# Two tiles for the blocks of w_down, loaded a unit ahead, the sums of g in the gate's places, and the sums pinned in program order on VectorE

## The chip, the core and the metric

The kernel runs on one core of one Trainium2 chip. The metric is the device time of one execution, in microseconds (us); lower is better. The kernel before takes 1152.91 us (median of 3 runs, 1152.59 to 1155.61). The engines are called as in the profile: PE is TensorE, PEld its weight loads, DVE is VectorE, ACT is ScalarE, POOL is GpSimd, SP is SyncE, which here issues all the DMAs from one queue, in order.

## What is computed

The reference runs one encoder layer on two sequences of 512 tokens (plus 16 meta tokens): a convolution branch and an attention branch, a projection `w_out`, and a gated feed-forward network (FFN). The change lies in the FFN alone:

```python
hf = _rms(h, ffn_norm_g[i])
h = h + (jax.nn.silu(hf @ w_gate[i]) * (hf @ w_up[i])) @ w_down[i]
```

`hf` has 1024 rows (tokens) and 1024 columns, `w_gate` and `w_up` are 1024 x 2816, `w_down` is 2816 x 1024. Everything is float32; the kernel gets that accuracy out of three matmuls on a high and a low part of each operand (`mm3`, L151).

## The kernel before

**Stages.** Projections and the convolution, attention, `w_out`, and then the FFN, in two parts: the *units* (gate and up), and the *down* products.

**Seven products in place of eight.** Each pair of 128-wide blocks of FFN columns is a 2 x 2 block product, and the kernel computes such a product by a scheme of Strassen's kind with 7 block products. It needs sums of the blocks of both operands. For a pair `p` (there are 11) unit `2p` makes the gate part `silu(hf @ w_gate)` and unit `2p+1` the up part, which is multiplied by the gate part at once; so there are 22 units of 7 products, 12 matmuls of 512 columns each. Before each product the block of weights or its sum is split into a high part (ACT, L962) and a low part (POOL, L964), in tiles `wc`; the sums of weight blocks themselves are made on DVE (L946, tiles `tt`, four of them). Each product leaves PE in a PSUM bank (`pt`, four of them), is read from there by ACT (L975) or DVE (L979, L981, L983, L993, L997) and so frees its bank; L998 multiplies by the gate part. `raw`, `h_...64` and a part of `slots` are the places to which the weights of gate and up units are loaded, two units ahead (L938).

**Sums for the down products.** The down product is done in the same way, with operands `g` (the result of gate and up) and `w_down`. Their sums are made while the units run, and go to DRAM:

- `g_sums(p, j)` (from L1003) runs in the up unit of pair `p`, and makes the sums of the four blocks of g: three written to the tiles `hf0` and `hf1` (`hf2` in the code, free since the FFN's transposes), one in place. DMAs store them to `d_a11s1`, `d_a12a22`, `d_s3s2` and `d_s4`.
- `w_sums(p, r, j)` (from L1021) handles the blocks of `w_down` for pair `p`, one half of the columns at a time (`r` = 0 in the up unit, `r` = 1 in the next pair's gate unit). One round is: load four 128 x 256 blocks into the tile `wt` (two DMAs, L1031), make four sums in place on DVE (L1035, L1037, L1040, L1042), store two of the blocks to `d_t1t3` (L1038) and two to `d_t4t2` (L1043). There are 22 rounds, and there is one `wt`: it has the place of the tile for the norm's gain (`tag="gain", bufs=1`), so that a round's loads wait for the stores of the round before.

**What sets the order.** The program is written for the Tile framework. Its scheduler places every instruction on its engine's queue by a simulation of the time at which its inputs are there, by what is ready, with the order of the program as the tie-break. The queue itself then runs strictly in order, and so does SP's queue of DMAs. The sums of `w_down` depend on nothing but their own loads, so that the scheduler may put them far ahead of the place in which the program has them. A place to which something is loaded or written is only waited for by semaphores; nothing else limits how far ahead it may be.

**Down products.** After the units, 77 steps of 12 matmuls read the stored sums back (L1117, L1118), split them (ACT L1129, DVE L1130) and multiply. They are split four steps ahead of their use and loaded eight steps ahead of that; the last units already prepare the first ones.

## Time and profile before

| | |
|---|---|
| Median of 3 runs | 1152.91 us (1152.59 to 1155.61) |
| Profiled execution: its own time | 1156.38 us |
| Profiled execution: span, first to last instruction | 1154.6 us |
| Granted TensorE clock, mean | 0.984 |
| PE busy, whole span | 1089.3 us (94%) |
| DVE busy, whole span | 837.4 us (73%) |
| DMA, mean | 127 GB/s |
| First load of `wt` and last one issued | 480.18 us, 726.02 us |
| Units: first product read from PSUM, last unit's first one | 468.22 us, 921.83 us |

How to read it: a line of the group view has the line of the kernel, the engine, the operation, what it writes and reads, the shape, the count, and then the busy time, the mean duration of one in ns, and the idle time just before with what ended it. A line of the timeline has the start, the duration, and in brackets the idle time of the engine before it. A row of the view by windows has, for each engine, its busy time in that stretch with the number of instructions, then the granted clock of PE (1.00 is full), the share of the DMA engines and the bytes moved. `xN` is always a count.

### The profile page before, as it was taken

How to read it: one execution, taken by the hardware profiler on the slowest of the kernel's cores; microseconds unless marked ns; L12 is line 12 of the kernel's file. 1: busy time of each engine (PE TensorE's matmuls, PEld its weight loads, DVE VectorE, ACT ScalarE, POOL GpSimd, SP SyncE). 2: the span in 40 equal slices, each digit the busy share in tenths (PEclk: the TensorE clock that was granted, in tenths of full speed). 3: DMA queues.
4: the chain of work that ended last, by engine and by line, in shares of the span. 5: the costliest groups of instructions: out<-in, count | busy, mean ns of one | idle time of the engine just before them, and what ended most of it. 6: DMA issues, size and time to landing. Idle time of an engine off the chain costs nothing.

```text
span 1154.6 us, 15888 instructions
## 1 busy us (share of the span) xinstructions
PE 1089.3 (94%) x5874; PEld 935.1 (81%) x5874; DVE 837.4 (73%) x1197; ACT 499.0 (43%) x832; POOL 471.5 (41%) x409
## 2 busy tenths in 40 slices
PE   5999998999999999789798998999999999999997
PEld 4999887888878999777576776888888888888886
DVE  5599997888887548997658678867675584756643
ACT  6455525786874525632221221333223344533431
POOL 6389736563652313583443434554554400000002
PEclk9999999999989999899998999999999999999999
DMA  8211111010111312445465465443314389765513
GB/s 277 76 38 41 42 52 55 25 56 1 38 37 64 120 37 92 139 143 183 140 216 193 144 209 170 150 137 117 120 39 135 126 308 369 250 224 183 183 37 127
DMA packets 71421, 147.06 MB, mean 127 GB/s; under 512 B 6944, under 2 KB 29728, under 8 KB 71344
## 3 DMA queue, kind: packets, MB, share of 16 engines
q1 hardware_dynamic: 71344, 146.06, 37.7%
q8 instruction: 46, 0.75, 0.3%
q14 instruction: 31, 0.25, 0.1%
HBM read 105.92 MB, written 40.11 MB: 126 GB/s over the span
## 4 chain that ended last, share of the span: by engine, by line
PE 59%; DVE 21%; DMA 12%; issue 3%; ACT 2%; POOL 1%; SPq 1%; DVEq 0%; POOLq 0%; ACTq 0%
PE pt L151 41%; PE ps L151 12%; DMA wt<-in_w_down_dram 5%; DMA d_t4t<-wt 5%; DVE ps L329 3%; DVE ps L337 3%; PE pt L645 2%; PE pt L615 2%; DVE pacc L339 1%; DVE wt L1037 1%; DVE wt L1035 1%; DVE tt L946 1%; DVE wt L1042 1%; DVE hf L879 1%; DMA raw<-in_w_in_dram 1%
## 5 line engine op out<-in xcount | busy, mean ns | idle before, releaser
L151 PE MATMUL pt<-act_h,wc 128*128 128x512 f32 (+1 forms) x552 | 178.2, 385 | 7.6 <-DVE slots L997 5.9
L964 POOL TENSOR_TENSOR wc<-tt,wc 128x512 fp32r<-128x512 f32 x84 | 114.9, 1386 | 99.2 <-ACT wc L962 78.0
L151 PE MATMUL pt<-hn_h,wp 128*128 128x256 f32 (+2 forms) x576 | 132.8, 324 | 1.1 <-ACT hn_h L141 1.1
L151 PEld LDWEIGHTS pt<-act_h,wc 128*128 128x128 f32 x552 | 104.2, 191 | 29.9 <-DVE slots L997 5.5
L176 POOL TENSOR_SCALAR ms<-ms 128x1 f32<-128x1 f32 (+1 forms) x24 | 12.8, 534 | 250.5 <-ACT re L175 213.8
L151 PE MATMUL pt<-act_l,wc 128*128 128x512 f32 (+1 forms) x276 | 106.3, 385 | 3.4 <-DVE act_l L898 3.4
L151 PEld LDWEIGHTS pt<-hn_h,wp 128*128 128x128 f32 x576 | 97.3, 192 | 10.1 <-ACT hn_h L141 1.5
L1130 DVE TENSOR_TENSOR re<-re,re 128x1024 fp32r<-128x1024 f32 x53 | 64.2, 1223 | 47.2 <-ACT re L1129 46.8
L151 PE MATMUL pt<-hn_l,wp 128*128 128x256 f32 (+2 forms) x288 | 93.6, 326 | 0.0
L137 POOL TENSOR_TENSOR wp<-raw,wp 128x1024 fp32r<-128x1024 f32 x28 | 69.2, 2472 | 54.9 <-ACT wp L134 54.8
L962 ACT CAST wc<-tt 128x512 fp32r<-128x512 f32 x88 | 51.2, 616 | 78.6 <-PE pt L151 69.9
L1129 ACT CAST re<-re 128x1024 fp32r<-128x1024 f32 x53 | 55.2, 1054 | 68.0 <-PE ps L151 23.8
L151 PE MATMUL pt<-re 128*128 128x512 f32 x360 | 84.0, 389 | 0.0
L151 PEld LDWEIGHTS pt<-re 128*128 128x128 f32 x360 | 67.6, 188 | 14.0
L964 POOL TENSOR_TENSOR wc<-raw,wc 128x512 fp32r<-128x512 f32 x30 | 42.1, 1419 | 79.8 <-ACT wc L962 79.8
L151 PE MATMUL pt<-a12h,wc 128*128 128x512 f32 (+1 forms) x184 | 63.7, 411 | 10.7 <-DVE slots L997 10.6
L151 PE MATMUL pt<-wp,act_h 128*128 128x256 f32 x384 | 71.4, 285 | 1.6 <-DVE h L842 1.5
L590 POOL TENSOR_SCALAR p<-p,sst 128x512 f32<-128x512 f32 x64 | 44.1, 693 | 69.3 <-DVE sst L588 61.3
L151 PE MATMUL pt<-s4h,wc 128*128 128x512 f32 (+1 forms) x184 | 60.1, 390 | 6.7 <-DVE h L979 6.7
L151 PEld LDWEIGHTS pt<-act_l,wc 128*128 128x128 f32 x276 | 53.0, 192 | 13.5 <-DVE act_l L898 3.6
L151 PE MATMUL ps<-re 128*128 128x512 f32 x276 | 63.9, 389 | 0.0
L151 PEld LDWEIGHTS pt<-wp,act_h 128*128 128x128 f32 x384 | 60.1, 192 | 2.2 <-DVE h L842 1.7
(283 smaller groups left out, 2895.8 us busy)
## 6 DMA issues: line engine op xcount, KB each, us to landing
raw<-in_w_gate_dram SPq DMA_DIRECT2D x22, 512.0 KB, 4.2
wt<-in_w_down_dram SPq DMA_DIRECT2D x44, 256.0 KB, 3.3
re<-in_w_down_dram SPq DMA_DIRECT2D x31, 256.0 KB, 4.6
raw<-in_w_in_dram SPq DMA_DIRECT2D x12, 512.0 KB, 3.8
slots<-in_w_up_dram SPq DMA_DIRECT2D x11, 512.0 KB, 3.7
d_t1t<-wt SPq DMA_DIRECT2D x22, 256.0 KB, 2.5
h<-in_w_up_dram SPq DMA_DIRECT2D x11, 512.0 KB, 5.7
d_t4t<-wt SPq DMA_DIRECT2D x22, 256.0 KB, 2.8
```

The source lines that it names most:

```text
L137: nc.gpsimd.tensor_sub(lo[:, a], raw[:, a], hi[:, a].bitcast(F32))
L151: nc.tensor.matmul(out_ap, lhsT=w_, rhs=m_, start=first and i + j == 0, stop=last and i == n - 1 and j == 2)
L176: nc.gpsimd.tensor_scalar(ms[:rows], ms[:rows], EPS, 0.0, op0=ALU.add, op1=ALU.add)
L329: nc.vector.scalar_tensor_tensor(a_, half_win(c, 0, i, HS + 1), k, a_, ALU.mult, ALU.add)
L337: nc.vector.scalar_tensor_tensor(m_, both[:, :, i:i + HS], k, m_, ALU.mult, ALU.add)
L590: nc.gpsimd.tensor_scalar(pr[:, real], pr[:, real], st[:, 2, t:t + 1], 1.0, op0=ALU.mult, op1=ALU.mult)
L615: nc.tensor.transpose(pt[:, t * 128:(t + 1) * 128], self.ps[t][:, n0:n0 + w], ident)
L645: nc.tensor.matmul(self.po, lhsT=v, rhs=p_, start=self.done + j == 1, stop=self.done + j == 5)
L962: nc.scalar.copy(w[:, 0:512], src)
L964: lo_eng.tensor_sub(w[:, 512:1024], src, w[:, 0:512].bitcast(F32))
L1129: nc.scalar.copy(w[:, :, LO], blocks[n])
L1130: nc.vector.tensor_sub(w[:, :, HI], blocks[n], w[:, :, LO].bitcast(F32))
```

## The change

- The blocks of `w_down` are loaded to `hf0` (rounds with `r` = 0) and `hf1` (`r` = 1), each 128 x 1024, in place of the one `wt`. The load is a function of its own, `w_load`, called after product 0 of each unit: that of `r` = 0 in the gate unit of its pair, that of `r` = 1 in the up unit. The sums that use it are one unit later, after products 1 to 4 (before: 3 to 6).
- `g_sums` writes its three sums to the places of the gate part (`half(4, 0)`, `half(4, 1)`, `half(0, 1)`: in `slots` and `h_...62`), which the up unit has consumed by then. The next gate unit writes these places again, after its products 4, 5 and 6.
- All sums of both kinds, and the loads of `w_load`, go through `in_order`: each is put behind the instruction that the program has just ahead of it on its engine's queue. The scheduler places all else as before.
- The tile of the norm's gain is no longer shared, so that the last gain can be loaded early.

The number of sums, loads and stores, and their sizes, stay the same.

```diff
     def g_sums(p, j):
 
         a11, a21, a12, a22 = half(3, 0), half(3, 1), half(7, 0), half(7, 1)
-        s3_, s2_, s4_ = hf2[0][:, 0:512], hf2[0][:, 512:], hf2[1][:, 0:512]
+        s2_, s3_, s4_ = half(4, 0), half(4, 1), half(0, 1)
         if j == 5:
-            nc.vector.tensor_sub(s3_, a11, a21)
-            nc.vector.tensor_add(a21, a21, a22)
+            in_order(nc.vector.tensor_sub(s3_, a11, a21))
+            in_order(nc.vector.tensor_add(a21, a21, a22))
             nc.sync.dma_start(d_a11s1[p], hres[3])
         elif j == 6:
             nc.sync.dma_start(d_a12a22[p], hres[7])
-            nc.vector.tensor_sub(s2_, a21, a11)
-            nc.sync.dma_start(d_s3s2[p], hf2[0])
+            in_order(nc.vector.tensor_sub(s2_, a21, a11))
+            nc.sync.dma_start(d_s2s3[p], hres[4])
         elif j == 7:
-            nc.vector.tensor_sub(s4_, a12, s2_)
+            in_order(nc.vector.tensor_sub(s4_, a12, s2_))
             nc.sync.dma_start(d_s4[p], s4_)
 
-    w_tile = {}
+    def w_cut(t, r):
+        return t.rearrange("p (i c) -> p i c", i=2)[:, :, r * 256:(r + 1) * 256]
+
+    def w_tile(r):
+        return hf2[r].rearrange("p (i c) -> p i c", i=4)
+
+    def w_load(p, r):
+        for i in range(2):
+            in_order(nc.sync.dma_start(w_tile(r)[:, 2 * i:2 * i + 2], w_cut(w_down[2 * p + i], r)))
 
     def w_sums(p, r, j):
...
-        if j == 0:
-            w_tile[0] = const.tile([P, 4, 256], F32, tag="gain", bufs=1, name=name("wt"))
-            for i in range(2):
-                nc.sync.dma_start(w_tile[0][:, 2 * i:2 * i + 2], cut(w_down[2 * p + i]))
-        w = w_tile[0]
+        w = w_tile(r)
         b11, b12, b21, b22 = (w[:, i] for i in range(4))
-        if j == 3:
-            nc.vector.tensor_sub(b11, b12, b11)
+        if j == 1:
+            in_order(nc.vector.tensor_sub(b11, b12, b11))
+        elif j == 2:
+            in_order(nc.vector.tensor_sub(b12, b22, b12))
+            nc.sync.dma_start(w_cut(d_t1t3[p], r), w[:, 0:2])
+        elif j == 3:
+            in_order(nc.vector.tensor_sub(b22, b22, b11))
         elif j == 4:
-            nc.vector.tensor_sub(b12, b22, b12)
-            nc.sync.dma_start(cut(d_t1t3[p]), w[:, 0:2])
-        elif j == 5:
-            nc.vector.tensor_sub(b22, b22, b11)
-        elif j == 6:
-            nc.vector.tensor_sub(b21, b21, b22)
-            nc.sync.dma_start(cut(d_t4t2[p]), w[:, 2:4])
+            in_order(nc.vector.tensor_sub(b21, b21, b22))
+            nc.sync.dma_start(w_cut(d_t4t2[p], r), w[:, 2:4])
...
         for j in range(7):
             u.product(j, slice(256, 512) if u.u == 0 else slice(0, 512))
+            if j == 0:
+                w_load(u.p, u.up)
```

`in_order(ins)` calls `tc.keep_in_program_order(ins)`. The new lines of the four sums are L1038, L1040, L1043 and L1045, those of the sums of g L1012, L1013, L1017 and L1020, the load is still L1031, and the stores are L1041 and L1046.

**Where instructions move, first place:** DVE in unit 3, an up unit, from the result of its product 1 (L997) on. Before:

```order
L997 TENSOR_TENSOR slots<-pt_5949,h_4063 128x512
L998 TENSOR_TENSOR slots<-slots,h_4062 128x512
L1035 TENSOR_TENSOR wt_6521<-wt_6521 128x256
L1037 TENSOR_TENSOR wt_6521<-wt_6521 128x256
L1040 TENSOR_TENSOR wt_6521<-wt_6521 128x256
L979 TENSOR_TENSOR h_4063<-pt_5966,h_4063 128x512
L1042 TENSOR_TENSOR wt_6521<-wt_6521 128x256
L946 TENSOR_TENSOR tt_6130<-slots,h_4064 128x512
L981 TENSOR_TENSOR slots<-pt_5987,h_4063 128x512
L946 TENSOR_TENSOR tt_6132<-slots,tt_6130 128x512
L1035 TENSOR_TENSOR wt_6671<-wt_6671 128x256
L983 TENSOR_TENSOR slots<-pt_6006,h_4063 128x512
```

Changed:

```order
L997 TENSOR_TENSOR slots<-pt_5948,h_4063 128x512
L998 TENSOR_TENSOR slots<-slots,h_4062 128x512
L1038 TENSOR_TENSOR hf_4705<-hf_4705 128x256
L979 TENSOR_TENSOR h_4063<-pt_5966,h_4063 128x512
L1040 TENSOR_TENSOR hf_4705<-hf_4705 128x256
L946 TENSOR_TENSOR tt_6131<-slots,h_4064 128x512
L981 TENSOR_TENSOR slots<-pt_5989,h_4063 128x512
L1043 TENSOR_TENSOR hf_4705<-hf_4705 128x256
L946 TENSOR_TENSOR tt_6133<-slots,tt_6131 128x512
L983 TENSOR_TENSOR slots<-pt_6008,h_4063 128x512
L997 TENSOR_TENSOR slots<-pt_6008,slots 128x512
L998 TENSOR_TENSOR slots<-slots 128x512
```

Before, three of the four sums of a round stand ahead of the result of product 2 (L979), and the first sum of the next round ahead of that of product 4 (L983): two rounds in one unit. Now each unit has one round, one sum behind each of the products 1 to 4; the fourth sum (L1045) is the row after the last one shown.

**Second place:** SP's queue at the end of that unit. Before, where `wt` is in its eighth round and then its ninth:

```order
L1031 DMA wt_6671<-in_w_down_dram 128x2x256 x2
L1038 DMA d_t1t_4031<-wt_6671 256x1x256
L1043 DMA d_t4t_4042<-wt_6671 256x1x256
L1031 DMA wt_6810<-in_w_down_dram 128x2x256 x2
L1012 DMA d_a12a_3996<-slots 128x1024
L1010 DMA d_a11s_3985<-slots 128x1024
L938 DMA raw_6075<-in_w_gate_dram 128x1024
L1014 DMA d_s3s_4007<-hf_4705 128x1024
L1017 DMA d_s_4018<-hf_4706 128x512
```

Changed:

```order
L1041 DMA d_t1t_4029<-hf_4705 256x1x256
L1046 DMA d_t4t_4040<-hf_4705 256x1x256
L1014 DMA d_a11s_3985<-slots 128x1024
L938 DMA raw_6074<-in_w_gate_dram 128x1024
L1016 DMA d_a12a_3996<-slots 128x1024
L1018 DMA d_s2s_4007<-slots 128x1024
L1031 DMA hf_4705<-in_w_down_dram 128x2x256 x2
L1021 DMA d_s_4018<-h_4062 128x512
L938 DMA h_4064<-in_w_up_dram 128x1024
```

Before, each load of `wt` stands directly behind the stores that it waits for, and the stores of the sums of g behind it. Now the load of a round comes three DMAs and more behind the stores that free its tile, and the sums that use it one unit later; at the end of unit 3 it is the third round that is stored, and not the eighth. On PE, ACT and POOL the rows of the units read the same before and after but for a few that are swapped around unit 0; in the down products some rows of PE and ACT stand in another order.

## The prediction

> **What bounds the kernel now.** I read the page first, for the engine that bounds, then the FFN by windows, then PE's waits there, and last DVE's timeline at one of them.

> ```profile
> PE 1089.3 (94%) x5874; PEld 935.1 (81%) x5874; DVE 837.4 (73%) x1197; ACT 499.0 (43%) x832; POOL 471.5 (41%) x409
> PE 59%; DVE 21%; DMA 12%; issue 3%; ACT 2%; POOL 1%; SPq 1%; DVEq 0%; POOLq 0%; ACTq 0%
> PE pt L151 41%; PE ps L151 12%; DMA wt<-in_w_down_dram 5%; DMA d_t4t<-wt 5%; DVE ps L329 3%; DVE ps L337 3%; PE pt L645 2%; PE pt L615 2%; DVE pacc L339 1%; DVE wt L1037 1%; DVE wt L1035 1%; DVE tt L946 1%; DVE wt L1042 1%; DVE hf L879 1%; DMA raw<-in_w_in_dram 1%
> 500.00:710.00 210.00, 185.90 (x767) 148.16 (x765) 149.55 (x211) 51.54 (x94) 93.78 (x69) 0.96 0.53 173
> 710.00:760.00 50.00, 49.51 (x212) 40.92 (x213) 40.85 (x54) 14.07 (x25) 23.47 (x17) 0.97 0.55 183
> 760.00:910.00 150.00, 150.00 (x663) 124.26 (x662) 102.81 (x120) 44.29 (x78) 76.47 (x56) 1.00 0.31 106
> 965.00:1140.00 175.00, 175.00 (x774) 144.96 (x773) 103.73 (x107) 68.96 (x74) 7.92 (x12) 1.00 0.57 192
> ```

> PE is the bound, but the second and third lines (the chain of waits by engine and by line) hold something that PE does not do: loads of `wt` and stores from it, 5% each, with DVE's sums between. The windows (in each row PE, PEld, DVE, ACT, POOL, then clock, DMA share, GB/s) say where. From 760 us on PE has no idle time and the full clock, and so it stays through the down products. Between 500 and 710 us it is idle for 24.1 of 210 us at a clock of 0.96. The same units are computed in both stretches.

> How much that costs is read best from the instant at which ACT takes product 0 of a unit from PSUM (L975). In even units nothing delays ACT there but PE:

> ```profile
> 488.15 0.37 ACT L975 COPY h<-pt 128x256 f32<-128x256 f32 x1
> 502.58 0.58 ACT L975 COPY h<-pt 128x512 f32<-128x512 f32 x1
> 525.48 0.59 ACT L975 COPY h<-pt 128x512 f32<-128x512 f32 x1 [1.69 <-issue]
> 570.95 0.59 ACT L975 COPY h<-pt 128x512 f32<-128x512 f32 x1 [1.58 <-issue]
> 617.68 0.59 ACT L975 COPY h<-pt 128x512 f32<-128x512 f32 x1 [1.58 <-issue]
> 662.78 0.59 ACT L975 COPY h<-pt 128x512 f32<-128x512 f32 x1 [1.58 <-issue]
> 707.71 0.59 ACT L975 COPY h<-pt 128x512 f32<-128x512 f32 x1 [1.58 <-issue]
> 750.46 0.59 ACT L975 COPY h<-pt 128x512 f32<-128x512 f32 x1 [1.58 <-issue]
> 788.54 0.59 ACT L975 COPY h<-pt 128x512 f32<-128x512 f32 x1 [1.58 <-issue]
> 902.78 0.59 ACT L975 COPY h<-pt 128x512 f32<-128x512 f32 x1 [1.58 <-issue]
> ```

> The first row is unit 0's second half, the second unit 1, then come units 2, 4, 6, 8, 10, 12, 14 and 20. From unit 14 to 20 three pairs take 114.24 us, 38.08 a pair: the pace that PE alone sets (168 matmuls of 0.227 us). The five pairs from 525.48 to 750.46 take 45.47, 46.73, 45.10, 44.93 and 42.75 us, 34.6 us more than five times 38.08. Unit 1 takes 22.90 us, 3.9 more than half a pair. That is the sum that can be won: 38.4 us.

> What ends the waits, by engine, and one of them in DVE's timeline:

> ```profile
> PE pt L151 <- DVE slots L997: 13.8, 8, 2.9
> PE pt L151 <- DVE h L979: 6.7, 5, 2.7
> DVE wt L1035 <- DMA wt<-in_w_down_dram: 43.2, 15, 6.0
> 705.88 1.39 DVE L1035 TENSOR_TENSOR wt<-wt 128x256 f32<-128x256 f32 x1 [2.26 <-DMA wt<-in_w_down_dram]
> 707.30 1.38 DVE L1037 TENSOR_TENSOR wt<-wt 128x256 f32<-128x256 f32 x1
> 708.72 0.42 DVE L1040 TENSOR_TENSOR wt<-wt 128x256 f32<-128x256 f32 x1
> 709.06 0.68 DVE L983 TENSOR_TENSOR slots<-pt,h 128x512 f32<-128x512 f32 x1
> 709.66 0.68 DVE L997 TENSOR_TENSOR slots<-pt,slots 128x512 f32<-128x512 f32 x1
> 710.49 0.77 PE L151 MATMUL pt<-a12h,wc 128*128 128x512 f32 x1 [2.86 <-DVE slots L997]
> ```

> (The first two rows are PE's waits from 440 to 710 us, the third DVE's from 480 to 710: us in total, times, longest.) DVE runs its queue in order, reaches the first sum of a round, and the blocks have not landed: 2.26 us here, 43.2 us over 15 rounds. Behind it stand the reads of finished products (L983, L997); the four PSUM banks are full, and PE waits until L997 frees one. The queue has the sums too early for one tile: a round is a closed loop of load, sums, store, next load.

> ```profile
> 480.18 1.32 SPq L1031 DMA_DIRECT2D wt<-in_w_down_dram  x2
> 726.02 1.25 SPq L1031 DMA_DIRECT2D wt<-in_w_down_dram  x2
> wt<-in_w_down_dram SPq DMA_DIRECT2D x44, 256.0 KB, 3.3
> ```

> The first and last loads of 22 rounds are 245.8 us apart, 11.7 us a round, and the units hold nearly two rounds each there, 23 us, where PE needs 19.04. When the rounds are used up, at about 735 us, the waits end.

> **The change part by part.**

> *The early rounds are spread.* One round per unit, its four sums behind products 1 to 4, the blocks loaded a unit ahead. A load takes 3.3 us and now has about 19. So the DVE waits on `wt` go (43.2 us in the rows), and with them what stood behind: 34.6 + 3.9 = 38.4 us of PE's pace. I take all of it, less what follows.

> *The low clock goes too.* Idle time is only 24.1 us of the first stretch and 0.5 of the second; the rest of the 38.4 is lost after the gaps:

> ```profile
> 518.07 0.50 PE L151 MATMUL pt<-s4h,wc 128*128 128x512 f32 x1 [1.99 <-DVE h L979]
> 518.00:522.40 4.40, 4.33 (x13) 3.38 (x14) 3.36 (x7) 0.00 (x0) 0.00 (x0) 0.64 0.43 155
> ```

> A gap of 1.99 us is followed by 4.4 us at a clock of 0.64, in which 12 matmuls take 4.3 us and not 2.7. [...]

> *The start of the units.* Six early sums stand on DVE between 486 and 502 us, and unit 1's second weight load stands on SP behind a store of `wt`:

> ```profile
> 487.95 0.57 SPq L1038 DMA_DIRECT2D d_t1t<-wt  x1
> 488.58 0.60 SPq L938 DMA_DIRECT2D h<-in_w_up_dram  x1
> ```

> In the changed order these sums are gone from there, and the load stands ahead of every store of sums. Four of the sums, 0.41 us each when alone (as L1040 above), come ahead of the splits for which PE waits: I take 1.5 us. At most it is what the stretch from 488.15 to 502.58 has over six products of 256 columns and one of 512 at PE's pace, 14.4 - (6 x 1.36 + 2.72) = 3.5 us. At least it is nothing.

> *The same sums now stand in all the other units.* In the clean stretch DVE had none. A sum costs 0.42 to 1.39 us, as the rows at 708.72 and 705.88 show; on average:

> ```profile
> 484.00:710.00 226.00, 54.52 (x79) 0.95 0.52 170
> 772.23:848.39 76.16, 76.16 (x338) 63.08 (x337) 51.56 (x60) 22.77 (x40) 38.40 (x29) 1.00 0.31 104
> 793.93 0.69 DVE L979 TENSOR_TENSOR h<-pt,h 128x512 f32<-128x512 f32 x1 [1.45 <-PE pt L151]
> 801.01 0.67 DVE L993 TENSOR_TENSOR slots<-pt,slots 128x512 f32<-128x512 f32 x1
> ```

> The first row is the sums on `wt` alone: 0.69 us each. Eight a pair add 5.5 us to the 25.8 us of the second row's pair (51.56 / 2): 31.3 of 38.08. DVE has had just that load: 40.85 of 50 us between 710 and 760, with PE busy for 49.51 of them. PE does not feel DVE's lateness before a bank is missing, which is three products or 8.2 us after a result is due, and DVE waits for PE again and again (third row, 1.45 us). So I cost this at nothing; uncovered it is 5.5 us a pair, the first rival. From below, nothing; a gain is excluded here, since PE has no idle time to give back.

> [...]

> *g's sums in the gate's places.* Same instructions and sizes. New is that the next gate unit's results of products 4 and 6 wait for the stores.

> ```profile
> 791.19 0.69 DVE L1016 TENSOR_TENSOR hf<-slots,hf 128x512 f32<-128x512 f32 x1
> d_s3s<-hf SPq DMA_DIRECT2D x11, 512.0 KB, 5.7
> ```

> The last sum of g ends at 791.9 before; four sums of 0.69 ahead of it make that about 794.7, and the store of 5.7 us lands at 800.4, as the result of product 4 is due (L993 at 801.01). Behind that L993 stand the reads of products 5 and 6 and of the next unit; with 8.2 us until a bank is missing, lateness of some us is hidden. Nothing.

> *SP's queue.* Four DMA issues of `w_load` move ahead or behind others, none is added. The loads now wait for stores issued at least three DMAs earlier, so that SP stands still less; the weight loads behind them come as early or earlier. Nothing. *After unit 21* DVE has eight more sums and SP about 2 MB more to move than before, at a stretch in which the down products have a lead of four steps (11 us) on DVE and twelve on the loads. At 0.69 us each the sums are 5.5 us, under the lead: 0 to 3 us, I take 1.

> *Sum.* 38.4 + 1.5 - 1 = 38.9; for the first units, where loads and splits still have to catch up, I keep back 2 us. 37 us less: span 1154.6 - 37 = 1117.6, own time of such an execution 1156.4 - 37 = 1119.4, and from the median 1152.9, which is 3.5 us below the profiled one, **1116 us**.

> **The rivals.**

> 1. *The sums slow the clean units: slower.* If DVE's idle 12.3 us a pair (38.08 - 25.8) is all in waits that recur after every delay, then each sum lengthens the pair, and and ten pairs may lose 39.9 us (38.4 + 1.5) before the kernel is slower: it decides at 4.0 us a pair, 0.5 us a sum. At 0.69 it costs 55 us, a time of 1168. For it: DVE waits for POOL and DMA too. Against it: nine sums between 710 and 734 us with PE busy throughout.
> 2. *Only idle time comes back.* If the clock from 500 to 710 us is low for another reason than the gaps, 24.6 + 1.5 - 3 = 23 us are won: 1130 us. Against it: 1.00 from 760 us on.
> 3. *A new wait takes the old one's place:* the store of g's sums, or SP held up behind a sum, costs some 2 us in each of ten pairs: 17 us are won, 1136 us. For it: 0.6 us of slack in the working above; against it the banks' 8.2 us.
> 4. *It doesn't do what it says:* the loads land late in spite of the order, since SP waits elsewhere, and PE waits as before: 1153 us. Against it: a load is issued some 19 us ahead of its sum.

> **How the numbers follow.** My forecast 77%, the rivals 4, 6, 10 and 3%. The forecast's own range is 1108 to 1124: the largest gain, 38.4 + 3.5, with nothing kept back, gives 1111, and 0.3% is what a measurement of this kernel can hardly tell from no change, 3 us; upwards another 8 us for the start and the down products. Taking in the second rival, the range is 1107 to 1132, and leaves out the first, the fourth and most of the third. Faster by over 0.3%: forecast and rivals 2 and 3, 93%; slower 4%, the same 3%.

> **What would show it.** Right: in the windows PE idle for under 4 us from 510 us to the units' end at a clock of 1.00; L975 of even units 38.1 us apart from unit 2 on; no wait of DVE for the loads of `hf0` and `hf1` in the waits; the load's lines gone from the chain; the last unit's product 0 at about 885 us and not 921.83. Wrong: pairs over 40 us with DVE without idle time (rival 1), a clock under 1.00 without gaps (2), L993 waiting for a DMA (3), sums waiting for their loads (4).

## The result and the profile after

The changed kernel takes 1117.2 us (median; 1116.52 to 1118.07), the kernel before 1152.75 us (1152.51 to 1155.61, four runs now). The ratio is 0.9686, with a 95% interval of 0.967 to 0.9703: 35.6 us less by the medians. The forecast was 1116 us, with a range of 1107 to 1132. The two profiled executions are further apart, 1156.38 and 1116.52 us, with spans of 1154.6 and 1114.7 us.

First the page of the changed kernel: busy time by engine, and the chain of waits by engine.

```profile
PE 1073.9 (96%) x5874; PEld 928.4 (83%) x5874; DVE 835.2 (75%) x1197; ACT 500.0 (45%) x832; POOL 472.8 (42%) x409
PE 77%; DVE 16%; ACT 3%; DMA 1%; issue 1%; POOL 1%; SPq 0%; POOLq 0%; ACTq 0%; DVEq 0%
```

DVE's work is the same (835.2 against 837.4 us). In the chain, DMA has gone from 12% to 1%: the loads of `wt` and the stores from it no longer set the end. PE has 15.4 us less of busy time with the same number of matmuls. The mean granted clock went from 0.984 to 0.994, so that some 12 of the 15.4 us are matmuls that took longer at the low clock before (an estimate: 1.6% of 1154.6 us less 0.6% of 1114.7).

Then the same units, and the first of the down products, by windows (PE, PEld, DVE, ACT, POOL, clock, DMA share, GB/s):

```profile
510.00:710.00 200.00, 200.00 (x884) 165.67 (x883) 153.70 (x204) 59.21 (x104) 100.74 (x75) 1.00 0.45 154
710.00:760.00 50.00, 50.00 (x222) 41.42 (x221) 38.20 (x52) 14.89 (x26) 26.14 (x19) 1.00 0.55 182
760.00:885.00 125.00, 125.00 (x553) 103.54 (x552) 90.03 (x120) 38.63 (x67) 60.62 (x45) 1.00 0.49 165
885.00:925.00 40.00, 40.00 (x178) 33.14 (x177) 32.86 (x41) 18.35 (x18) 0.00 (x0) 1.00 0.96 344
```

From 510 to 925 us PE is busy without a gap at the full clock. The instant at which ACT takes product 0 of units 1, 2, 20 and 21 from PSUM, in ACT's timeline:

```profile
501.26 0.57 ACT L975 COPY h<-pt 128x512 f32<-128x512 f32 x1
520.22 0.59 ACT L975 COPY h<-pt 128x512 f32<-128x512 f32 x1 [1.58 <-issue]
862.94 0.59 ACT L975 COPY h<-pt 128x512 f32<-128x512 f32 x1 [1.58 <-issue]
881.99 0.59 ACT L975 COPY h<-pt 128x512 f32<-128x512 f32 x1 [1.42 <-PE pt L151]
```

From unit 2 to unit 20 nine pairs take 342.72 us, 38.08 a pair, and unit 1 takes 18.96. Where the 39.9 us between the two spans lie can be read from the same rows of both kernels: units 1 to 21 take 380.73 us (881.99 - 501.26) and took 419.25 (921.83 - 502.58), 38.5 us less. The stretch from unit 0's second half to unit 1 gave 0.8 us, the time ahead of it 0.6, and the rest after unit 21 0.1 (232.7 us in both).

Last, the two longest of PE's waits between 440 and 930 us, and the three longest of DVE's between 480 and 885 us (us in total, times, longest):

```profile
PE pt L151 <- DVE act_l L898: 3.4, 1, 3.4
PE px L890 <- ACT act_h L897: 1.9, 1, 1.9
DVE slots L997 <- issue: 31.7, 9, 3.5
DVE tt L946 <- POOL wc L964: 29.6, 26, 1.2
DVE h L979 <- PE pt L151: 10.8, 19, 0.8
```

The last of PE's waits there, 0.94 us, ends at 496.31 us, still in unit 0. No row of DVE names a load of `hf`, where 43.2 us stood on `wt`; DVE now waits for PE, for POOL, once for a load of the down products (3.6 us), or for nothing that the profile shows.

### The profile page after: what moved, and what is told of

Same layout as the page of the kernel before. It is cut to its first block, busy times and chain, and to the rows that moved or that the text cites. A ratio compares the mean times of both kernels' runs of the same rounds, so it can differ in the third digit from the quotient of the medians.

```text
span 1114.7 us, 15902 instructions
## 1 busy us (share of the span) xinstructions
PE 1073.9 (96%) x5874; PEld 928.4 (83%) x5874; DVE 835.2 (75%) x1197; ACT 500.0 (45%) x832; POOL 472.8 (42%) x409
## 3 DMA queue, kind: packets, MB, share of 16 engines
q1 hardware_dynamic: 71344, 146.06, 38.4%
## 4 chain that ended last, share of the span: by engine, by line
PE 77%; DVE 16%; ACT 3%; DMA 1%; issue 1%; POOL 1%; SPq 0%; POOLq 0%; ACTq 0%; DVEq 0%
PE pt L151 58%; PE ps L151 13%; DVE ps L329 3%; DVE ps L337 3%; PE pt L645 3%; PE pt L615 2%; DVE pacc L339 1%; DVE hf L879 1%; PE px L240 1%; DVE wc L964 1%; ACT p L587 1%; DVE act_l L898 1%; DMA raw<-in_w_in_dram 1%; DVE tt L946 0%; DVE cq_l L142 0%
## 5 line engine op out<-in xcount | busy, mean ns | idle before, releaser
L151 PE MATMUL pt<-act_h,wc 128*128 128x512 f32 (+1 forms) x552 | 176.2, 382 | 0.1
L964 POOL TENSOR_TENSOR wc<-tt,wc 128x512 fp32r<-128x512 f32 x84 | 117.7, 1417 | 106.6 <-ACT wc L962 60.0
L151 PE MATMUL pt<-hn_h,wp 128*128 128x256 f32 (+2 forms) x576 | 132.4, 323 | 1.1 <-ACT hn_h L141 1.1
L151 PEld LDWEIGHTS pt<-act_h,wc 128*128 128x128 f32 x552 | 103.4, 190 | 19.8 <-issue 0.3
L151 PE MATMUL pt<-act_l,wc 128*128 128x512 f32 (+1 forms) x276 | 105.6, 383 | 3.7 <-DVE act_l L898 3.4
L151 PEld LDWEIGHTS pt<-hn_h,wp 128*128 128x128 f32 x576 | 97.0, 191 | 10.1 <-ACT hn_h L141 1.5
L151 PE MATMUL pt<-hn_l,wp 128*128 128x256 f32 (+2 forms) x288 | 93.5, 325 | 0.0
L151 PE MATMUL pt<-re 128*128 128x512 f32 x360 | 84.0, 389 | 0.0
L151 PEld LDWEIGHTS pt<-re 128*128 128x128 f32 x360 | 67.6, 188 | 14.0
L151 PE MATMUL pt<-wp,act_h 128*128 128x256 f32 x384 | 71.4, 285 | 1.6 <-DVE h L842 1.5
L151 PEld LDWEIGHTS pt<-act_l,wc 128*128 128x128 f32 x276 | 52.4, 190 | 13.9 <-DVE act_l L898 3.6
L151 PE MATMUL ps<-re 128*128 128x512 f32 x276 | 63.9, 389 | 0.0
L151 PEld LDWEIGHTS pt<-wp,act_h 128*128 128x128 f32 x384 | 60.1, 192 | 2.1 <-DVE h L842 1.7
L307 POOL TENSOR_TENSOR pacc<-pacc,prod 128x512 f32<-128x512 f32 x43 | 58.3, 1356 | 7.0 <-ACT prod L305 4.3
L151 PEld LDWEIGHTS ps<-re 128*128 128x128 f32 x276 | 51.8, 188 | 10.7
## 6 DMA issues: line engine op xcount, KB each, us to landing
raw<-in_w_gate_dram SPq DMA_DIRECT2D x22, 512.0 KB, 4.3
hf<-in_w_down_dram SPq DMA_DIRECT2D x44, 256.0 KB, 4.0
re<-in_w_down_dram SPq DMA_DIRECT2D x31, 256.0 KB, 5.3
raw<-in_w_in_dram SPq DMA_DIRECT2D x12, 512.0 KB, 3.9
slots<-in_w_up_dram SPq DMA_DIRECT2D x11, 512.0 KB, 3.5
h<-in_w_up_dram SPq DMA_DIRECT2D x11, 512.0 KB, 5.6
d_t1t<-hf SPq DMA_DIRECT2D x22, 256.0 KB, 5.5
d_t4t<-hf SPq DMA_DIRECT2D x22, 256.0 KB, 2.5
```

The lines of the kernel that those rows point to most:

```text
L151: nc.tensor.matmul(out_ap, lhsT=w_, rhs=m_, start=first and i + j == 0, stop=last and i == n - 1 and j == 2)
L307: nc.gpsimd.tensor_add(acc, acc, to)
L964: lo_eng.tensor_sub(w[:, 512:1024], src, w[:, 0:512].bitcast(F32))
```

## The experiments

The change has four parts: the w sums pinned on DVE, a second tile, loads a unit ahead (pinned on SP), and g's sums in other places and pinned. The runs take them apart. Two theories stood against each other at first. Q: what counts is where the sums stand on DVE's queue, one round per unit. T: what counts is the second tile with the early load, which lets the blocks land in time.

### The pins alone

```diff
-            nc.vector.tensor_sub(b11, b12, b11)
+            in_order(nc.vector.tensor_sub(b11, b12, b11))
   (and the three other sums alike; one tile wt, the rest as before)
```

> The kernel before with one edit: the four sums of a round of w_down are pinned in program order on DVE. One tile wt, its loads directly behind its own stores, and g's sums in hf, all as before. On DVE's queue each unit now has one round. Theory Q (the queue): the loss came from sums that stand on DVE ahead of their loads, two rounds a unit; a round's loop takes 11.7 us and a unit 19.04, so that one tile is enough once the rounds are paced: 1115 to 1120 us, pairs 38.1 us apart, DVE waits on the loads of wt under 5 us in all. Rival T (the tile): the second tile and the load a unit ahead are what takes the wait away; with one tile the load of a round is issued only behind the store of the round before, DVE still waits for it, some 2 us a unit, of which half reaches PE: 1130 to 1140 us.

Measured: 1129.86 us (1128.54 to 1131.73), ratio 0.9806 (0.9791 to 0.982). That is just under two thirds of the gain; Q as put, 1115 to 1120 us, was too strong, and T's 1130 to 1140 us was missed by 0.1 us. The rounds stand one per unit, yet one tile costs 12.7 us. The first sum of some of the rounds on DVE's timeline, and two of PE's waits for DVE:

```profile
648.94 0.42 DVE L1038 TENSOR_TENSOR wt<-wt 128x256 f32<-128x256 f32 x1 [4.62 <-DMA wt<-in_w_down_dram]
664.61 0.41 DVE L1038 TENSOR_TENSOR wt<-wt 128x256 f32<-128x256 f32 x1
688.70 0.43 DVE L1038 TENSOR_TENSOR wt<-wt 128x256 f32<-128x256 f32 x1 [6.19 <-DMA wt<-in_w_down_dram]
768.32 0.43 DVE L1038 TENSOR_TENSOR wt<-wt 128x256 f32<-128x256 f32 x1 [7.09 <-DMA wt<-in_w_down_dram]
809.10 0.43 DVE L1038 TENSOR_TENSOR wt<-wt 128x256 f32<-128x256 f32 x1 [6.51 <-DMA wt<-in_w_down_dram]
...
770.69 0.47 PE L151 MATMUL pt<-a12h,wc 128*128 128x512 f32 x1 [1.98 <-DVE slots L993]
811.47 0.47 PE L151 MATMUL pt<-a12h,wc 128*128 128x512 f32 x1 [2.43 <-DVE slots L993]
```

DVE waits for the load in every second round, some 5 to 7 us. Up to 730 us PE does not notice, not even a wait of 6.19 us: even units stay 38.08 us apart. Behind each of the later waits, of 7.09, 6.51, 6.30 and 7.49 us, PE has a gap of 1.6 to 2.4 us, and the pairs of units around the first three are 40.0 to 40.8 us long. The length of the wait alone does not decide that. Counted from product 0 of their unit (ACT's L975, 673.60 and 749.75 us for the rounds at 688.70 and 768.32), the waits without a gap end after 13.4 to 15.9 us and those with one after 18.3 to 19.1: the slack of the banks ends between 15.9 and 18.3 us. DVE comes to the later rounds later, since the last sum of the round ahead begins 3.1 us after product 0 in the first case and 7.8 in the second. The wait itself is the turn of the one tile: the last sum of a round begins at 757.58 us, its store is issued at 758.11, the load that overwrites what the store reads at 763.19, and the first sum of the next round runs at 768.32, 10.7 us after the last. At the end, the rounds behind unit 21 wait once more, and PE has one gap of 3.5 us in the down products.

### The tiles without the pins

```diff
     def in_order(ins):
-        tc.keep_in_program_order(ins)
+        return ins
   (otherwise the changed kernel)
```

> The changed kernel without any pin (in_order returns its instruction as it is): two tiles, g's sums in the gate's places, and the scheduler free to place sums and loads. On DVE's queue the 22 rounds then stand within the first six units, three or four to a unit. Theory Q: a round's loop of 11.7 us, with two tiles 5.9 us a round, allows 3.2 rounds in 19.04 us; DVE again reaches sums whose blocks have not landed, and PE waits in units 1 to 6, some 3 to 5 us in each, and no more after: 1128 to 1145 us. Rival T: with two tiles a load lands while the other tile is summed, and the wait is gone wherever the sums stand: 1115 to 1120 us.

Measured: 1149.43 us (1147.05 to 1152.06), ratio 0.9967 (0.9953 to 0.9981). T falls: second tile and loads that the program issues a unit ahead bring 0.3% by themselves. Q's range, 1128 to 1145, was missed too. The scheduler gathers the rounds in front even more than before, 22 rounds in units 0 to 6, and two tiles are used up as one was. DVE's and PE's waits between 480 and 700 us:

```profile
DVE hf L1040 <- DMA hf<-in_w_down_dram: 16.0, 11, 3.6
DVE hf L1038 <- DMA hf<-in_w_down_dram: 10.8, 9, 2.9
PE pt L151 <- DVE slots L997: 11.9, 6, 5.2
PE pt L151 <- DVE h L979: 9.0, 4, 3.9
```

DVE waits less for loads (26.8 us) than before, but it has up to four rounds a unit to do; all 35 us are lost by unit 9, after which the units are 19.04 us apart.

### The sums of g in the gate's places alone

```diff
-        s3_, s2_, s4_ = hf2[0][:, 0:512], hf2[0][:, 512:], hf2[1][:, 0:512]
+        s2_, s3_, s4_ = half(4, 0), half(4, 1), half(0, 1)
   (with the store and its reader; otherwise the kernel before)
```

> The kernel before with the sums of g in the gate's places and nothing else: one tile wt, no pins. Its DVE queue has the rounds where the kernel before has them. Theory Q: no effect of its own, 1150 to 1156 us. Rival (the places matter by themselves, by a store that no longer holds hf or one that now holds the gate's result): over 5 us either way.

Measured: 1153.16 us, ratio 0.9997 (0.9979 to 1.0015). The places cost and bring nothing; they only free `hf0` and `hf1` for the tiles.

### The kernel before, once more

> The kernel before once more, for a second profile. Its runs lie between 1152.5 and 1156.4 us and the changed kernel's within 1.6 us. If the waits of PE for DVE vary from one execution to the next, since they hang on when loads land, the units' stretch (product 0 of unit 1 to that of unit 21, 419.25 us in the first profile) differs by some us and the rest of the span does not. If it is something else, the other stretches differ.

Measured: 1151.85 us, span 1150.1. Product 0 of units 1 and 21:

```profile
501.76 0.57 ACT L975 COPY h<-pt 128x512 f32<-128x512 f32 x1
917.31 0.59 ACT L975 COPY h<-pt 128x512 f32<-128x512 f32 x1 [1.42 <-PE pt L151]
```

Units 1 to 21 take 415.55 us here and took 419.25 in the first profile: of the 4.5 us between the two spans, 3.7 lie in the stretch that the change repairs. In 19 runs beside the first of these experiments the kernel before took 1149.43 to 1155.32 us; the changed kernel stays within 1.6 us. The waits themselves hardly differ. That stretch as one window, in the first profile and in this one:

```profile
502.58:921.83 419.25, 394.66 (x1682) 321.02 (x1681) 294.00 (x382) 112.69 (x202) 196.22 (x143) 0.98 0.45 148
501.76:917.31 415.55, 390.61 (x1682) 317.40 (x1681) 292.53 (x382) 112.58 (x201) 196.40 (x143) 0.99 0.44 149
```

PE is idle for 24.6 us in the first and 24.9 in the second; the 1682 matmuls of both rows take 394.66 and 390.61 us. The granted clock is at 0.50 for 20.5 us in the first and for 10.2 in the second. So the difference is in how often the clock is low behind the gaps; the last section shows what went with that in the first profile.

### Which of the other parts are needed

From here on the theory, P, had two conditions: DVE must meet one round per unit, and the blocks must land before its first sum or not much later, for which the tile needs time for its turn. A second tile is one way to have that time. R: a second tile or a load a unit ahead is needed. First, loads in the unit of their sums instead of a unit ahead:

```diff
-            if j == 0:
-                w_load(u.p, u.up)
+            if j == 0 and u.u:
+                w_load(*divmod(u.u - 1, 2))
   (and the last load after unit 21)
```

> The changed kernel, but the blocks of a round are loaded after product 0 of the unit whose sums use them (first sum behind product 1), not a unit ahead; two tiles and pins stay. Theory P (what counts is that DVE meets one round per unit, and that the blocks land before, or not much later than, the first sum; the banks give PE 8.2 us of slack): DVE waits up to 4 us on the load once per unit, PE none: 1115 to 1120 us. Rival R (the lead of a whole unit is needed, since any wait on DVE that stands in every unit reaches PE): 1122 to 1140 us, PE waits for DVE's reads of product 1 and 2 in each unit.

Measured: 1116.6 us (1116.05 to 1117.22), ratio 0.9702 (0.9688 to 0.9717), as the changed kernel. DVE does wait for the load, and longer than the 4 us that P expected:

```profile
DVE hf L1038 <- DMA hf<-in_w_down_dram: 35.0, 12, 5.7
```

That is up to 5.7 us, 35.0 us in all. The window from 510 us shows PE without a gap:

```profile
510.00:710.00 200.00, 200.00 (x884) 165.62 (x883) 156.71 (x205) 58.68 (x104) 102.80 (x74) 1.00 0.45 154
```

So 43.2 us of DVE waits on the load before and 35.0 here look much alike in a table of waits, and cost 38 us and nothing. It matters only whether a single delay goes past the slack.

Second, program order kept for the four w sums alone, loads and sums of g free:

```diff
-            in_order(nc.vector.tensor_sub(s3_, a11, a21))
+            nc.vector.tensor_sub(s3_, a11, a21)
   (likewise g's other sums and the loads)
```

> The changed kernel with program order kept for the four sums of w_down's blocks alone; the loads on SP's queue and the sums of g are placed freely by the scheduler. Theory P: 1115 to 1119 us, as changed, since the rounds stand one per unit on DVE by their own pins. Rival S (the pins on the loads or on the sums of g carry part of the gain): 1122 us or more.

Measured: 1117.58 us (1114.8 to 1117.76), ratio 0.9705 (0.9688 to 0.9722). The other pins do nothing.

Third, one tile, g's sums in their old places, the w sums pinned but packed behind products 3 and 4, which leaves the tile two products more for its turn:

```diff
         if j == 3:
             in_order(nc.vector.tensor_sub(b11, b12, b11))
-        elif j == 4:
             in_order(nc.vector.tensor_sub(b12, b22, b12))
             nc.sync.dma_start(cut(d_t1t3[p]), w[:, 0:2])
-        elif j == 5:
+        elif j == 4:
             in_order(nc.vector.tensor_sub(b22, b22, b11))
-        elif j == 6:
             in_order(nc.vector.tensor_sub(b21, b21, b22))
             nc.sync.dma_start(cut(d_t4t2[p]), w[:, 2:4])
```

> The kernel before (one tile, sums of g in their old places) with the four sums of a round pinned, but packed: the first two behind product 3, the last two behind product 4 instead of 3, 4, 5, 6. The turn of the one tile (last sum, store out of it, next load into it, first sum) then has two products or 5.4 us more. Theory P (the pinned kernel with one tile loses time only because its turn of 9 to 10 us, 4.1 us a store and 4.2 us a load, is as long as what it has between two rounds): no DVE wait on the load beyond 3 us, 1115 to 1121 us. Rival R (a second tile or a load a unit ahead is needed): 1126 to 1134 us, as with the sums spread out (1129.9).

Measured: 1115.74 us (1114.52 to 1117.86), ratio 0.9697 (0.9679 to 0.9714). R falls: one tile does what two do. SP's timeline and DVE's at one turn:

```profile
761.27 0.57 SPq L1044 DMA_DIRECT2D d_t4t<-wt  x1
763.79 1.25 SPq L1034 DMA_DIRECT2D wt<-in_w_down_dram  x2
760.84 0.41 DVE L1043 TENSOR_TENSOR wt<-wt 128x256 f32<-128x256 f32 x1
775.30 0.41 DVE L1038 TENSOR_TENSOR wt<-wt 128x256 f32<-128x256 f32 x1
```

And DVE's waits on the load, all of them from 480 to 930 us:

```profile
DVE wt L1038 <- DMA wt<-in_w_down_dram: 1.6, 1, 1.6
```

From the last sum to the next first one there are 14.5 us where the spread sums left 10.7 with a wait of 7.1 in them; the load is issued 11.5 us ahead of its sum. This and the changed kernel cannot be told apart by time, but it needs neither a second tile nor other places for g's sums.

Fourth, the same packing without the pins:

```diff
-        tc.keep_in_program_order(ins)
+        return ins
```

> The packed sums in one tile (1115.7 us when pinned) without the pins. Theory P (both are needed: the pin, which makes DVE meet one round per unit, and the time between two rounds): the scheduler gathers the rounds of units 1 to 21 in units 0 to 11 as in the kernel before, DVE waits 30 us or more for loads, 1140 to 1155 us. Rival T (the packing alone does it; the pin only sets the order among sums that would fit anyway): 1115 to 1125 us.

Measured: 1153.17 us (1149.22 to 1156.77), ratio 1.0002 (0.9986 to 1.0018). DVE's wait on the load is back:

```profile
DVE wt L1038 <- DMA wt<-in_w_down_dram: 45.9, 15, 6.0
```

The scheduler puts the rounds into units 0 to 10, as in the kernel before, whatever the program says. Both conditions of P are needed: as before, or with packed sums alone, 1153 us; with two tiles alone 1149; with the pins alone 1130; with the pins and either of the two 1116 to 1118.

### What is left of the cover

```diff
+            in_order(nc.vector.tensor_sub(spare[:, 0], b12, b11))
             in_order(nc.vector.tensor_sub(b11, b12, b11))
   (each of the four sums likewise done twice)
```

> The changed kernel with each of the four sums of a round done a second time into a spare tile just ahead of the real one: 88 sums of 128x256 more on DVE, some 0.63 us each, 2.5 us a unit. Theory P (sums of which the blocks have landed hide behind PE: DVE is busy 27.4 of 38.08 us a pair, and 32.4 with these): 1115 to 1120 us. The prediction's first rival (what is added to DVE in a clean unit slows the unit): 2.5 us in each of 21 units or part of it, 1135 to 1170 us.

Measured: 1126.37 us (1124.61 to 1127.46), ratio 0.9786 (0.9767 to 0.9804), 9 us more than the changed kernel. Neither side had it right. The window that answers to the first one above:

```profile
500.00:700.00 200.00, 198.78 (x874) 163.46 (x873) 189.15 (x237) 58.02 (x106) 107.93 (x74) 1.00 0.46 157
```

And PE's waits from 502 to 890 us:

```profile
PE pt L151 <- DVE slots L997: 2.7, 9, 0.3
```

DVE is busy 189.15 of 200 us, against 153.70: 6.7 us more a pair for eight sums, 0.84 us of DVE's time for each and not the 0.63 of a sum in the changed kernel. Of these 6.7 us, 0.5 reach PE (nine pairs of 38.57 us and not 38.08, product 0 of unit 2 at 520.87 and of unit 20 at 868.02), in gaps of 0.3 us that leave the clock at 1.00. Some 4 us more are lost after unit 21 (887.63 to 1124.4, 236.8 us and not 232.7). So the cover of the sums ends somewhere between 77% of DVE, where the changed kernel stands (153.70 of 200 us), and the 95% of this run.

### What a late read costs PE

DVE was held up by spare sums of 128x512 ahead of its read of product 1 (L996 in these kernels), in six units:

```diff
             elif j == 1:
+                for _ in range(HOLD.get(self.u, 0)):
+                    in_order(nc.vector.tensor_sub(spare[:, 0:512], half(1, 1), half(5, 0)))
+                in_order(nc.vector.tensor_copy(spare[:, 512:513], bk[:, 0:1])) if self.u in HOLD else None
                 self.result(0, 0, bk, "p1", cs)
   (HOLD has the number of spare sums by unit; the copy of one column pins the read behind them)
```

> The changed kernel with DVE held up by 12, 14, 16, 19, 22 and 26 spare sums of 128x512 ahead of its read of product 1 in units 4, 7, 10, 13, 16 and 19 (0.6 to 0.7 us each, about 7 to 17 us in all). What a late sum costs PE: theory P, with 8.2 us of slack in the banks: nothing in units 4 and 7, then idle time of PE that grows by what is added, 0 to 9 us a unit. [...]

Measured: 1194.27 us. PE idles in each of the six units, 6.54 us in the first and 16.0 in the last; I had expected nothing there and 9 us at most. DVE's and PE's timeline around the first:

```profile
561.66 9.03 DVE L978 TENSOR_TENSOR spare<-h,slots 128x512 f32<-128x512 f32 x7
571.21 3.58 DVE L978 TENSOR_TENSOR spare<-h,slots 128x512 f32<-128x512 f32 x5
575.52 0.79 PE L151 MATMUL pt<-act_h,wc 128*128 128x512 f32 x1 [6.54 <-DVE h L996]
```

And the windows behind that gap:

```profile
575.50:577.50 2.00, 1.98 (x5) 1.60 (x6) 2.00 (x4) 0.63 (x1) 0.00 (x0) 0.50 0.00 0
577.50:579.50 2.00, 2.00 (x7) 1.57 (x6) 2.00 (x6) 0.00 (x0) 0.00 (x0) 0.53 0.14 49
```

Seven spare sums beside POOL take 9.03 us, five without it 3.58; my 0.6 to 0.7 us was the time of a sum alone. PE's last product-1 matmul runs from 560.43 to 560.82 us, and its gap begins at 575.52 - 6.54 = 568.98, so the slack of three products, 8.2 us, is as costed. The unit loses 8.6 us, 2.1 more than its gap: two 2 us windows behind the gap run at a clock of 0.50 and 0.53. None of the six gaps is shorter than 6 us, so they don't show what a gap of about 2 us does to the clock, hence a second run with fewer sums, in eight units.

> The hold again with fewer spare sums, for idle times between 0 and 5 us: 7, 8, 3, 4, 5, 6, 7 and 8 sums ahead of the read of product 1 in units 3, 5, 8, 10, 12, 14, 16 and 18. With 12 sums PE stood idle for 6.54 us in unit 4, from 8.3 us after the last matmul of product 1, so by about 0.69 us a sum less: some 0.3 to 4 us here, in rising order from unit 8 to unit 18. Theory C (any idle time of PE over about 1.5 us is followed by a low clock): the granted clock in the 4 us behind the idle time is below 1.00 for idle times of 2 us too, and these units lose more than their idle time, by some 1 to 2.5 us. [...] Theory P alone: 1125 to 1140 us in all.

Measured: 1128.1 us. It had just three gaps, where I had expected six or more, in PE's timeline:

```profile
603.08 0.47 PE L151 MATMUL pt<-act_h,wc 128*128 128x512 f32 x1 [0.50 <-DVE slots L1000]
801.10 0.50 PE L151 MATMUL pt<-act_h,wc 128*128 128x512 f32 x1 [1.74 <-DVE h L996]
844.23 0.80 PE L151 MATMUL pt<-act_h,wc 128*128 128x512 f32 x1 [4.74 <-DVE h L996]
```

A window of 2 us behind each of the two longer ones:

```profile
803.00:805.00 2.00, 2.00 (x10) 1.64 (x10) 2.00 (x3) 0.00 (x0) 2.00 (x2) 1.00 0.02 6
846.00:848.00 2.00, 2.00 (x6) 1.52 (x6) 2.00 (x5) 0.00 (x0) 0.00 (x0) 0.50 0.47 162
```

After 1.74 us the clock stays at 1.00, after 4.74 us it is 0.50 for about 6 us. This contradicts C's 1.5 us, but there is no gap between 1.74 and 4.74 us. Such gaps are in the kernel before, in the last section.

## Why the prediction was right, and where its steps were off

**What bounds, and the 38.4 us.** Right: units 1 to 21 gave 38.5 us. The reading of product 0's instants in even units was the whole sum; a count of PE's idle time would have missed a third of it. All the marks named beforehand are in the profile: no gap from 510 us to the units' end, clock 1.00, 38.08 us a pair, no DVE wait on `hf`, no load of `hf` in the chain, and product 0 of the last unit at 881.99 us (885 forecast).

**The mechanism.** Partly right. "The queue has the sums too early for one tile" named both conditions, but the step "*The early rounds are spread*" gave the credit to the early load ("A load takes 3.3 us and now has about 19"). The runs show that neither the 19 us nor the second tile is needed. Loads in the unit of their sums do as well (1116.6), and so does one tile with packed sums (1115.7). What the change could not do without is the order on DVE.

**The low clock goes too.** Right in the sum; as the reason for all that is not idle time it was too wide. PE's waits in units 1 to 21 before are 24.6 us of the 38.5. Of the other 13.9 the low clock accounts for some 10.2 (an estimate: half of the 20.5 us that it lasted at 0.50). The remaining 3.7 us are in neither figure. A gap cost more than its length at the full clock too: nine gaps of 2.7 us in all made nine pairs 4.4 us longer in the run with doubled sums, 0.2 us a gap. For the 15 gaps of the kernel before that makes 3 us (an estimate from that run). Rival 2, that only idle time comes back (1130 us), falls. One run of the study happens to lie at 1130, the pins alone, but for another reason.

**The start of the units.** Taken at 1.5 us, measured 0.8, within the bounds of 0 to 3.5.

**The sums in the other units.** Costed at nothing, and nothing it was; the working was too high. A sum takes 0.63 us on average (0.45 to 0.91 by line) and not 0.69. In the two pairs for which the prediction read 51.56 us of DVE, the changed kernel has

```profile
772.23:848.39 76.16, 76.16 (x337) 63.08 (x336) 58.39 (x77) 22.78 (x40) 38.57 (x28) 1.00 0.47 159
```

That is 29.2 us a pair (58.39 / 2) and not 31.3, also because other subtractions became shorter (from 760 to 885 us `tt<-slots` in L946 takes 677 ns where it took 1773). Rival 1 priced each added sum at its whole length once DVE's waits recur. The doubled sums show that the waits do absorb: of 6.7 us added a pair, 0.5 reached PE.

**g's sums and SP's queue.** Costed at nothing, and nothing it was: 0.9997 for g's places alone, no gap of PE at L993. Rival 3 had its price from the 0.6 us of slack. It did not come to that: L993 waits for PE (2.0 and 1.1 us in DVE's waits) and never for a store, so the banks' slack was not needed here. Rival 4 falls with the DVE waits.

**After unit 21.** Taken at -1 us, measured 0.1 us the other way: 232.7 us in both kernels. DVE did the eight more sums, and the DMA share was 0.96 between 885 and 925 us, without a gap of PE.

**Kept back for the first units.** The 2 us were not needed: from unit 1 on the units are at PE's pace.

**From the span to the median.** This step was wrong, and it hid the others. The terms gave a span of 1117.6 us, and 1114.7 were measured, 2.9 less. Then 3.5 us were taken off because the profiled execution of before lay that far above its median. But those 3.5 us are no property of the chip or the start that both kernels share. Of the 4.5 us between two executions of before, 3.7 lie in units 1 to 21; they are part of the loss that was already counted in the 38.4, and so were subtracted twice. The two errors of about 3 us have opposite signs, and 1116 came out 1.2 us from 1117.2: luck in the number, beside a mechanism that held.

## What to carry to other kernels

Where an in-order engine both frees the bottleneck's buffers and does side work on loaded data, a scheduler that places the side work early can put a short-lived buffer's load turn in front of those reads; pin the side work at the pace of the bottleneck, and leave between two uses of its buffer as much time as store and reload take. A second buffer is not the only way to get that time: packing the users closer does the same. Read such a loss from the spacing of one event per iteration on the bottleneck, not from idle time or from a table of waits, since 35 us of waits below the slack cost nothing here, and 24.6 us of gaps went with a loss of 38.5.

## What the hardware showed that was not expected

```profile
565.13 0.50 PE L151 MATMUL pt<-s4h,wc 128*128 128x512 f32 x1 [2.69 <-DVE h L979]
515.84:519.25 3.41, 1.42 (x7) 1.01 (x6) 3.38 (x6) 0.00 (x0) 0.83 (x1) 1.00 0.71 278
519.25:522.66 3.41, 3.41 (x10) 2.63 (x9) 2.11 (x4) 0.01 (x1) 0.00 (x0) 0.50 0.35 108
560.21:563.62 3.41, 2.23 (x10) 1.50 (x8) 2.41 (x2) 0.75 (x2) 3.41 (x3) 1.00 0.86 250
563.62:567.03 3.41, 1.90 (x8) 1.60 (x9) 3.38 (x7) 0.00 (x0) 0.12 (x1) 1.00 0.33 113
567.03:570.44 3.41, 3.41 (x16) 2.83 (x16) 0.18 (x1) 1.14 (x2) 1.51 (x2) 1.00 0.37 121
```

The gap of 1.99 us lies in one cell, in which PE was busy for the other 1.42 us, and the next cell has the clock at 0.50. The gap of 2.69 us is split over two cells, 1.18 and 1.51 us, and the clock stays at 1.00. (The 0.64 of the prediction's row is a mean over full and half.) From 500 to 930 us of this trace PE is idle for 1.80, 1.99, 2.22, 2.22, 2.67 and 2.77 us in six cells, and behind each of them is a cell at 0.50; in every other cell it is idle for 1.63 us or less, and none of those is followed by a low one. In the run with the pins alone gaps of 1.98 and 2.43 us (PE's rows at 770.69 and 811.47) leave the mean clock from 760 to 900 us at 1.00. So theory C's 1.5 us is refuted as a rule for a gap's length; in the trace of the kernel before, what goes with the low clock is how much idle time falls into one cell. This is read from the trace as it fell; no run moved a gap on purpose. That the same sets the two profiled executions of the kernel before apart (24.6 and 24.9 us idle, 20.5 and 10.2 us at 0.50) is my estimate and is not shown here.

Also not expected: a DVE sum took longer while POOL was busy beside it. The same spare sum took 1.29 us (9.03 / 7, from 561.66 us on; POOL is busy for 6.13 of the 12 us from 560 to 572) and, a few us later, 0.72 (3.58 / 5, from 571.21 us on; POOL has 0.00 from 572 to 576). In the kernel before, L1035 and L1037 took 1.39 and 1.38 us while POOL was busy from 705.69 to 708.41 us, and L1040, right behind, 0.42. Why DVE comes to the rounds later in the later units of the run with the pins alone is not settled: its waits are longer there, 6.3 to 7.5 us, but the time from the last sum of a round to the first of the next is not (9.9 to 10.7 us, and 8.3 to 12.0 up to 730 us).
